# Attention weights times values: one block at a time, or four in one run, in a hybrid encoder layer

## The chip, the core and the metric

The kernel runs on one NeuronCore of a Trainium2 chip. The metric is the device time of one execution in microseconds (us). The core has a matrix engine (TensorE, PE in the profile; its weight loads are PEld), VectorE (DVE), ScalarE (ACT), GpSimd (POOL) and SyncE (SP), which issues nearly all transfers. Each engine works through its own list of instructions in order and waits on semaphores for the others.

## What is computed

The layer takes x of 1024 tokens by 1024 features and puts 16 learned meta tokens in front. Cut to what matters:

```python
u = _rmsnorm(h, norm_g[l])
z = u @ w_in[l]
gq, gk, gv, r_f, r_b, g_gate, nq, nk, nv, n_gate = jnp.split(z, split_at, axis=-1)
...  # gated linear attention (GLA) of 4 heads, one scan in each direction -> o_gla
qn = _rmsnorm(nq.reshape(B, L, NA_HEADS, NA_HEAD_DIM), q_norm_g[l])
kn = _rmsnorm(nk.reshape(B, L, NA_HEADS, NA_HEAD_DIM), k_norm_g[l])
# neighbourhood attention (NA), 16 heads of 64, per grid row of 64 tokens:
s_loc = jnp.einsum('bchd,bicjhd->bhcij', q_r, k_g) * scale   # + position bias
s_meta = jnp.einsum('bchd,bmhd->bhcm', q_r, km) * scale + mb
p = jax.nn.softmax(jnp.concatenate([s_loc.reshape(B, H, W, wh * ww), s_meta], axis=-1), axis=-1)
o = (jnp.einsum('bhcij,bicjhd->bchd', p_loc, v_g) + jnp.einsum('bhcm,bmhd->bchd', p_meta, vm))
o_na = o * jax.nn.silu(n_gate)
h = h + jnp.concatenate([o_gla, o_na], axis=-1) @ w_out[l]
```

The change touches the last product of the neighbourhood attention, weights p times values.

## The kernel before

The program has a front stage with the neighbourhood attention and a second stage with the GLA scans and the output projection. All dense products are made in a three-part form (`mm3`, L409 to L412: high by high, high by low, low by high half of each operand), so one step of 128 features is three matmuls.

**Neighbourhood attention.** The 1024 tokens are regrouped into 8 blocks of 16 grid rows by 8 columns. The 16 heads are taken as 8 pairs, numbered 0 to 7; two heads of 64 fill the 128 rows. `attn(p)` (L771) does one pair. After `k_prep` (L681), which transposes the keys (kmt, kt) and makes their halves, it goes through nine steps s = 0 to 8 (L858). In step s it

- transposes the finished weights of unit s-1 (`transposes`, L818): waits for the normalization on DVE (`norm`, L807; L814 writes P), makes three PE transposes for each of the two heads (tile pp, L825), and copies them to PT, head 0 on ACT (L829), head 1 on DVE (L831);
- starts unit s (`softmax`, L781): scores of query block s on PE (`qk`, tile s, L763 and L764), bias and row maximum on DVE (L791), exponentials on ACT (L797, L798), and the normalization deferred by 1500 and 2100 ns;
- in odd steps prepares the next two query blocks (`q_prep`, L721: PE transposes into qt, ACT copies L730, DVE L737 and POOL L741 for the other half);
- lets the dense stream run to a point inside the step (t0), then multiplies weights and values of unit s-1 (`pv`, L835), then lets the dense stream run to the end of the step (t1).

`pv` makes six matmuls, L844, from three key blocks and two heads. Each head's result has 64 rows, so head 0 uses one half of the array's columns and head 1 the other. The profile shows each of these float32 matmuls as two records, twelve for a unit. The third key block is a tile of 16 meta rows (kvm) in units 0 and 7, and VM otherwise, where the meta rows lie in the places of some tokens. Four units share one PSUM bank (po); after the fourth, L854 on DVE multiplies the bank by the gate tile ng, whose silu (ACT L648 to L651, POOL L652) is called in at the latest there (`finish(gate_rest)`, L851).

**What sets the order.** The order of instructions is made when the program is built, by `Sched` (L70). It counts ns of tensor work. The attention is the main thread; the dense stream of the next pair (`dense_na`, tiles pn_na; meta tokens pm_na; gates pz_na) is the filler, which is drawn in between by ("gap", ns) and ("to", position), and `defer` puts work of other engines a given number of ns of tensor work later. `STEP_AT` and `PV_AT` (L38, L39) place the steps and the products in the filler. ("w", 710) after `pv` says that the product counted as 710 ns. Beside the last pair runs the dense stream of the first GLA head (pz_gz, pn_gv).

**Dense evacuation.** A finished pn_na bank is read by ACT (L546, L548, L549: square, q and k, v); DVE reduces the square (L551), POOL makes the reciprocal root (L212, L213), DVE applies it (L556). Weights are split into halves by ACT and POOL (L253, L254) or DVE alone (L256, L257).

**Transfers by GpSimd.** In the GLA stage each head loads its values back with two transfers from GpSimd's queue (L1033, L1034).

Of the kernel before, what the change touches and what calls it, by code (L numbers as in the profile page):

```python
# [8 lines left out]
F32 = mybir.dt.float32  # L9
# [5 lines left out]
PSUM = bass.MemoryType.PSUM  # L15
# [11 lines left out]
# emission distances in ns of tensor work  # L27
# [9 lines left out]
LAST_NS = 3438.0  # L37
PV_AT = (0.5, 0.5, 0.5, 0.6, 0.5, 0.5, 0.5, 0.5)  # L38
# [12 lines left out]
# emission positions of block 0's parts, 8 * token block + feature block  # L51
# [8 lines left out]
# evacuations of halves that DVE does alone  # L60
# [4 lines left out]
# of four weight pieces, which ACT and Pool split  # L65
# [4 lines left out]
class Sched:  # L70
    """Orders the emission: a main thread, a filler thread and deferred work."""
# [10 lines left out]
    def defer(self, ns, fn):  # L82
        """Emits fn after ns more of tensor work, or when the returned handle is called."""
        state = []

        def once():
            if not state:
                state.append(1)
                fn()

        self.n += 1
        heapq.heappush(self.heap, (self.pe + ns, self.n, once))
        return once
# [46 lines left out]
def kernel(  # L140
# [27 lines left out]
    nc = tc.nc  # L168
# [22 lines left out]
    def pt_tile(name, hold):  # L191
        """the single bank of short-lived products, expected to be free again after hold ns."""
        S.pt_free = S.pe + hold
        return ps_tile("pt", name, 1)
# [5 lines left out]
    # ------------------------------------------------------------- constants  # L200
# [4 lines left out]
    rs = con.tile([128, 8], F32, name="rs")  # L205
# [4 lines left out]
    def rstd(dst, ss, inv_n, eng_n):  # L210
        """dst = (ss * inv_n + eps) ** -0.5 on tiny tiles."""
        pool.tensor_scalar(dst, ss, inv_n, EPS, OP.mult, OP.add)  # L212
        pool.tensor_tensor(dst, dst, epsm[: dst.shape[0], :eng_n], OP.pow)  # L213

    # ------------------------------------------------------------- weights
    pieces = []

    def add_block(key, aps, pack=1):
        """a block's pieces: each holds `pack` of its [128, columns] parts."""
        pieces.extend((key, i, pack, a) for i, a in enumerate(aps))  # L220
# [55 lines left out]
    def release(ns=0.0):  # L276
        """a piece has had its last use: the next one takes its place ns later."""
        allowed[0] += 1
        S.defer(ns, lambda: pump() if nsplit[0] < allowed[0] else None)

    # ------------------------------------------------------------- u^T
# [5 lines left out]
    # ------------------------------------------------------------- NA pools  # L287
# [20 lines left out]
    def x_load(b):  # L308
        """token block b with its features on the partitions."""
        xs[b] = zt_tile(f"x{b}")  # L310
        if b > 0:
            sp.dma_start(xs[b], xt[b])
# [5 lines left out]
    def x_rows(b):  # L318
        """token block b with its tokens on the partitions."""
        xr[b] = flat(VM if b % 2 else xv)  # L320
        sp.dma_start(xr[b], xn[b])
# [17 lines left out]
    def u_part(b, k):  # L339
        """both parts of feature block k of u^T, short of the tokens' rstd."""  # L340
        xk = xs[b][:, k * 128 : k * 128 + 128]
        ts = slice(b * 128, b * 128 + 128)
        g = gT[:, k : k + 1]
        act.activation(uh[:, k, ts], xk, AF.Copy, scale=g)
        dve.scalar_tensor_tensor(ul[:, k, ts], xk, g, f32(uh[:, k, ts]), OP.mult, OP.subtract)

    def u_split(b):
        """both parts of token block b of u^T, short of the tokens' rstd."""
        ts = slice(b * 128, b * 128 + 128)
        x3 = xs[b].rearrange("p (k t) -> p k t", k=NKB)  # L350
        halves = (slice(0, 4), slice(4, 8))
        for ks in halves:
            dve.tensor_tensor(x3[:, ks], x3[:, ks], gT[:, ks, None].to_broadcast([128, 4, 128]), OP.mult)
        for ks in halves:
            act.activation(uh[:, ks, ts], x3[:, ks], AF.Copy)  # L355
        for ks in halves:
            dve.tensor_tensor(ul[:, ks, ts], x3[:, ks], f32(uh[:, ks, ts]), OP.subtract)  # L357

    def u_rstd(b):
        """the tokens' rstd: a column of rs."""  # L360
        st = nap.tile([128, 2], F32, tag="ust", name=f"ust{b}", bufs=2)
        for i in range(2):
            junk = ps_tile("ps", f"junk{b}_{i}", 2)
            act.activation(junk, xr[b][:, 512 * i : 512 * i + 512], AF.Square, accum_out=st[:, i : i + 1])
        dve.tensor_tensor(st[:, 0:1], st[:, 0:1], st[:, 1:2], OP.add)
        rstd(rs[:, b : b + 1], st[:, 0:1], 1.0 / 1024, 1)
# [7 lines left out]
    def u_spread(b):  # L374
        """the tokens' rstd: on the free axis of all partitions."""
        ps = ps_tile("ps", f"rb{b}", 2)
        pe.matmul(ps[:, 0:128], ones, dg[b], start=True, stop=True)
        act.activation(rbc[:, b * 128 : b * 128 + 128], ps[:, 0:128], AF.Copy)
        S.adv(220)

    def u_meta():
        """um: both parts of the meta tokens' u^T."""
# [25 lines left out]
    # ------------------------------------------------------------- dense parts  # L408
# [5 lines left out]
    def first_pair(key, c1, hook):  # L414
        """token blocks 0 and 1 of the first weight block, each piece used for both as it comes."""
        ps = [ps_tile("pd", f"pn_{key[0]}{key[1]}_{b}", 2) for b in range(2)]
        for i, (b, k) in enumerate(FIRST):
            u_part(b, k)
            if (key, k) not in split:
                pump()  # L420
            hook(i)
            wh, wl, _ = split[(key, k)]
            cs = slice(b * 128, b * 128 + 128)
            mm3(ps[b][:, :c1], uh[:, k, cs], ul[:, k, cs], wh[:, :c1], wl[:, :c1], k == 0, k == NKB - 1)
            yield 3 * c1 / 2.4
        return ps

    def natural(key, b, c0, c1, pump_last=False, hooks={}, spread=0.0, tag=("pd", 2)):
        """psum[tok' of block b, columns c0:c1 of the weight block]; yields costs, returns the bank."""
# [14 lines left out]
    def transposed(key, c0, evac, pump_last=False, lag=LAG):  # L444
        """psum[128 columns from c0, 512 tokens tok'] of both halves, the second behind the first."""
# [26 lines left out]
    def seq_view(ap):  # L472
        """a [p, 1024] row-major token view, iterated in tok' order (block, row, column)."""
        return ap.rearrange("p (r b c) -> p b r c", r=16, b=8, c=8)
# [13 lines left out]
    # ------------------------------------------------------------- NA static operands  # L488
# [42 lines left out]
    # ------------------------------------------------------------- dense stream of the NA pairs  # L531
# [114 lines left out]
    def swish(g, e, ns):  # L646
        """g *= 1 / (1 + exp(-g)), with e for the second factor; the steps ns after the first."""
        act.activation(e, g, AF.Exp, scale=-1.0)  # L648
        return [
            S.defer(ns[0], lambda: act.activation(e, e, AF.Ln, bias=1.0)),  # L650
            S.defer(ns[1], lambda: act.activation(e, e, AF.Exp, scale=-1.0)),  # L651
            S.defer(ns[2], lambda: pool.tensor_tensor(g, g, e, OP.mult)),  # L652
        ]

    def run_silu():
        """the pending gates."""
# [16 lines left out]
    # ------------------------------------------------------------- neighbourhood attention  # L673
    vm_scr = dram.tile([NPAIR, 16, 128], F32, name="vm_scr")

    def v_load(p):
        """values of pair p with the meta rows in the places of each block's last column of tokens."""
# [3 lines left out]
    def k_prep(p):  # L681
        """key operands of pair p."""
# [70 lines left out]
    def span(u):  # L753
        """first block and score columns of the unit of query block u."""
        return (0 if u == 0 else u - 1), (272 if u in (0, 7) else 416)
# [15 lines left out]
    def attn(p):  # L771
# [5 lines left out]
        po = {}  # L777
        f0 = S.fill
# [39 lines left out]
        def transposes(u, Ps, norm):  # L818
            ch = ((0, 128), (144, 128), (128, 16) if u in (0, 7) else (288, 128))
            PT = []  # L820
            for a in range(2):
# [4 lines left out]
                t = nap.tile([128, 384], F32, tag="PT", name=f"PT{p}{u}{a}", bufs=4)  # L826
# [31 lines left out]
        for s in range(9):  # L858
# [19 lines left out]
            if PT is not None:  # L878
# [3 lines left out]
                pv(pu, PT)  # L882
                yield ("w", 710)
# [4 lines left out]
    # ------------------------------------------------------------- GLA: dense streams  # L888
# [5 lines left out]
    def dense_gz(h):  # L894
        """q^T and k^T of head h in row-major token order, and k^T of the meta tokens."""
# [21 lines left out]
    def r_prep():  # L917
        """[rh; rl; rh] rows of both directions' decay ranks, tokens row-major, then meta."""
# [30 lines left out]
    def dense_gv(h):  # L949
        """v of head h (bounced to row-major token order), with the decay ranks in head 0's block."""  # L950
# [42 lines left out]
    # ------------------------------------------------------------- GLA: the scans  # L993
# [29 lines left out]
    def gla(h):  # L1023
# [128 lines left out]
        def state(d, n):  # L1152
            """the chunk's own contribution k~^T v, in PSUM."""
# [116 lines left out]
    # ------------------------------------------------------------- output projection  # L1270
# [64 lines left out]
    # ------------------------------------------------------------- the whole  # L1335
# [144 lines left out]
```

## Time and profile before

| | |
|---|---|
| time, median of 3 runs | 1182.36 us (1178.92 to 1186.05) |
| profiled execution, span from first to last instruction | 1179.6 us; no other time of that execution is given |
| mean granted TensorE clock | 0.991 |
| DMA | 99.35 MB, 84 GB/s mean |

How to read it: a row of the timeline gives start and length in us, the engine, the line, the operation, the tile written and those read, the shape, and in brackets the idle time in front with what ended it. Matmuls overlap in the pipeline, so the distance between two starts tells what one costs, not its length. Equal neighbours are put in one row with their count (x4); the length is then from the first start to the last end.

### The profile page before, as it was taken

How to read it: one execution, taken by the hardware profiler on the slowest of the kernel's cores; microseconds unless marked ns; L12 is line 12 of the kernel's file. 1: busy time of each engine (PE TensorE's matmuls, PEld its weight loads, DVE VectorE, ACT ScalarE, POOL GpSimd, SP SyncE). 2: the span in 40 equal slices, each digit the busy share in tenths (PEclk: the TensorE clock that was granted, in tenths of full speed). 3: DMA queues.
4: the chain of work that ended last, by engine and by line, in shares of the span. 5: the costliest groups of instructions: out<-in, count | busy, mean ns of one | idle time of the engine just before them, and what ended most of it. 6: DMA issues, size and time to landing. Idle time of an engine off the chain costs nothing.

```text
span 1179.6 us, 18996 instructions
## 1 busy us (share of the span) xinstructions
PE 1134.1 (96%) x6739; PEld 984.9 (83%) x6739; DVE 796.3 (68%) x1995; ACT 523.2 (44%) x1363; POOL 408.0 (35%) x477
## 2 busy tenths in 40 slices
PE   9899999999999999999999799899989999999998
PEld 7789898988989898897897689689868977787876
DVE  6966767776676777677646876865576587756352
ACT  6655565655646565564544333431442144212110
POOL 4743625343352534334205332531333222202010
PEclk9999999999999999999999899999999989999999
DMA  8620303012040301203126023303512454324132
GB/s 266 212 65 2 124 2 117 10 51 75 2 124 2 117 9 52 73 2 104 36 73 192 27 75 89 123 18 91 150 30 71 119 178 147 97 56 129 49 105 106
DMA packets 74414, 99.35 MB, mean 84 GB/s; under 512 B 6672, under 2 KB 45328, under 8 KB 74320
## 3 DMA queue, kind: packets, MB, share of 16 engines
q1 hardware_dynamic: 70096, 89.75, 24.8%
q0 software_dynamic: 4224, 8.39, 2.4%
q8 instruction: 53, 0.87, 0.3%
q14 instruction: 41, 0.34, 0.1%
HBM read 72.89 MB, written 21.04 MB: 80 GB/s over the span
## 4 chain that ended last, share of the span: by engine, by line
PE 76%; DVE 14%; issue 3%; ACT 3%; POOL 2%; DMA 1%; SPq 0%; POOLq 0%; DVEq 0%; ACTq 0%
PE pn_na L410 7%; PE pn_na L411 6%; PE pn_na L412 6%; PE pout L410 4%; PE pout L412 4%; PE pout L411 4%; PE po L844 4%; PE pp L825 3%; DVE ga L1072 3%; PE pn_gv L410 3%; PE pn_gv L412 3%; PE pn_gv L411 3%; PE pz_na L410 2%; PE pz_na L412 2%; PE pz_na L411 2%
## 5 line engine op out<-in xcount | busy, mean ns | idle before, releaser
L410 PE MATMUL pn_na<-wh,uh 128*128 128x384 f32 x512 | 180.3, 352 | 0.4 <-ACT uh L355 0.3
L254 POOL TENSOR_TENSOR wl<-raw,wh 128x512 fp32r<-128x512 f32 (+2 forms) x97 | 131.2, 1366 | 128.9 <-ACT wh L253 95.6
L411 PE MATMUL pn_na<-wl,uh 128*128 128x384 f32 x512 | 174.0, 340 | 1.2 <-POOL wl L254 1.0
L412 PE MATMUL pn_na<-wh,ul 128*128 128x384 f32 x512 | 173.3, 338 | 0.1
L410 PE MATMUL pout<-wh,oh 128*128 128x512 f32 x256 | 104.4, 408 | 6.6 <-DVE acc L1331 3.6
L410 PEld LDWEIGHTS pn_na<-wh,uh 128*128 128x128 f32 x512 | 96.1, 188 | 9.0 <-issue 7.8
L412 PE MATMUL pout<-wh,oh 128*128 128x512 f32 x256 | 102.1, 399 | 0.0
L411 PE MATMUL pout<-wl,oh 128*128 128x512 f32 x256 | 102.0, 398 | 0.0
L411 PEld LDWEIGHTS pn_na<-wl,uh 128*128 128x128 f32 x512 | 96.3, 188 | 3.6 <-POOL wl L254 2.5
L412 PEld LDWEIGHTS pn_na<-wh,ul 128*128 128x128 f32 x512 | 96.1, 188 | 0.9 <-DVE ul L357 0.7
L1331 DVE TENSOR_TENSOR acc<-acc,pout 128x512 f32<-128x512 f32 x64 | 43.8, 684 | 63.7 <-PE pout L412 63.6
L797 ACT ACTIVATE P<-P,sm 128x384 f32<-128x384 f32 x96 | 58.5, 609 | 51.9 <-DVE sm L794 51.9
L410 PE MATMUL pn_gv<-wh,uh 128*128 128x256 f32 (+1 forms) x256 | 76.3, 298 | 0.0
L253 ACT ACTIVATE wh<-raw 128x512 fp32r<-128x512 f32 (+2 forms) x97 | 57.5, 608 | 37.6 <-PE pout L412 18.8
L412 PE MATMUL pn_gv<-wh,ul 128*128 128x256 f32 (+1 forms) x256 | 73.0, 285 | 0.0
L411 PE MATMUL pn_gv<-wl,uh 128*128 128x256 f32 (+1 forms) x256 | 72.9, 285 | 0.0
L212 POOL TENSOR_SCALAR post<-post 128x1 f32<-128x1 f32 x32 | 6.5, 203 | 190.5 <-ACT on L1207 190.4
L791 DVE CUSTOM_DVE_ANT_0 P<-s,wt 128x416 f32<-128x416 f32 (+1 forms) x128 | 69.5, 543 | 2.5 <-PE s L764 2.5
L213 POOL TENSOR_TENSOR ss<-ss,epsm 128x4 f32<-128x4 f32 x64 | 68.9, 1077 | 5.3
L814 DVE TENSOR_SCALAR P<-P,sm 128x384 f32<-128x384 f32 (+1 forms) x128 | 66.9, 522 | 4.5
L212 POOL TENSOR_SCALAR ss<-ss 128x4 f32<-128x4 f32 x64 | 14.1, 221 | 157.7 <-DVE ss L551 96.3
L410 PEld LDWEIGHTS pout<-wh,oh 128*128 128x128 f32 x256 | 48.6, 190 | 19.7 <-DVE gt L483 3.3
(359 smaller groups left out, 3057.9 us busy)
## 6 DMA issues: line engine op xcount, KB each, us to landing
raw<-in_w_na_dram SPq DMA_DIRECT2D x56, 256.0 KB, 2.8
v_scr<-gvst SPq DMA_DIRECT2D x64, 128.0 KB, 2.3
raw<-in_w_o_dram SPq DMA_DIRECT2D x32, 256.0 KB, 2.9
oin<-o_scr SPq DMA_DIRECT2D x32, 256.0 KB, 3.1
v<-v_scr POOLq DMA_DIRECT2D x4, 1536.0 KB, 9.2
VM<-vnat SPq DMA_DIRECT2D x8, 512.0 KB, 4.5
o_scr<-ng SPq DMA_DIRECT2D x8, 512.0 KB, 3.5
raw<-in_w_gz_dram SPq DMA_DIRECT2D x16, 256.0 KB, 2.7
```

The costliest lines, as they stand in the source:

```text
L213: pool.tensor_tensor(dst, dst, epsm[: dst.shape[0], :eng_n], OP.pow)
L253: act.activation(wh[:, :n], r[:, :n], AF.Copy)
L254: pool.tensor_tensor(wl[:, :n], r[:, :n], f32(wh[:, :n]), OP.subtract)
L410: pe.matmul(ps, ah, bh, start=start, stop=False)
L411: pe.matmul(ps, ah, bl, start=False, stop=False)
L412: pe.matmul(ps, al, bh, start=False, stop=stop)
L791: dve.tensor_tensor_reduce(P[:, :n], ps[:, :n], wt[2 * p + a][:, off : off + n], 1.0, -3.0e38, OP.add, OP.max, mx)
L797: act.activation(loc, loc, AF.Exp, bias=mx, accum_out=sm[:, a : a + 1])
L814: dve.tensor_scalar(loc, loc, r, None, OP.mult)
L825: pe.transpose(pp[:w, c * 128 : c * 128 + 128], Ps[a][0][:, c0 : c0 + w], ident)
L844: pe.matmul(po[0][64 * a : 64 * a + 64, u4 * 128 : u4 * 128 + 128], V[:, 64 * a : 64 * a + 64], PT[a][:w, c * 128 : c * 128 + 128], start= ...
L1331: dve.tensor_tensor(a, a, ps, OP.add)
```

## The change

- `attn` collects the finished units in a list, `ready`, and calls `pv` for four of them in one run when the list is full, in steps 4 and 8. The run counts as 4 x 654 + 56 ns of tensor work.
- The pool for PT has eight buffers instead of four.
- The program is built with a scratch of 4096 bytes for descriptors of GpSimd's transfers, instead of the default.

Comments and docstrings were taken out as well, so line numbers move a little.

```diff
+PV_BATCH = 4
...
         po = {}
+        ready = []
...
-                t = nap.tile([128, 384], F32, tag="PT", name=f"PT{p}{u}{a}", bufs=4)
+                t = nap.tile([128, 384], F32, tag="PT", name=f"PT{p}{u}{a}", bufs=8)
...
                 if s == 1:
                     for m in vload:
                         m()
-                pv(pu, PT)
-                yield ("w", 710)
+                ready.append((pu, PT))
+                if len(ready) == PV_BATCH:
+                    for r in ready:
+                        pv(*r)
+                    yield ("w", 654 * PV_BATCH + 56)
+                    ready.clear()
             if s < 8:
                 yield ("to", t1)
...
-    nc = _bacc.Bacc("TRN2", target_bir_lowering=False, num_devices=1)
+    nc = _bacc.Bacc("TRN2", target_bir_lowering=False, num_devices=1, dynamic_dma_scratch_size=4096)
```

On PE, in step 5 of the first pair, the program before had unit 4's product (L844, tile po) between matmuls of the dense stream (pn_na_5):

```order
L410 MATMUL pn_na_5_1335<-wh_699,uh 128x384
L411 MATMUL pn_na_5_1335<-wl_700,uh 128x384
L412 MATMUL pn_na_5_1335<-wh_699,ul 128x384
L844 MATMUL po_1358<-PT_1294,vnat_137 64x128
L844 MATMUL po_1358<-PT_1300,vnat_137 64x128
L844 MATMUL po_1358<-PT_1294,vnat_137 64x128
L844 MATMUL po_1358<-PT_1300,vnat_137 64x128
L844 MATMUL po_1358<-PT_1294,VM 64x128
L844 MATMUL po_1358<-PT_1300,VM 64x128
L410 MATMUL pn_na_5_1335<-wh_713,uh 128x384
```

Now the dense matmuls there follow each other, and the products stand in runs; this is the middle of the run in step 4 of the same pair, on PE, from the end of unit 0 over unit 1 to the start of unit 2 (kvm holds the meta values, VM and vnat values of tokens):

```order
L847 MATMUL po_1251<-PT_948,kvm_639 64x128
L847 MATMUL po_1251<-PT_955,kvm_639 64x128
L847 MATMUL po_1251<-PT_1036,vnat_137 64x128
L847 MATMUL po_1251<-PT_1042,vnat_137 64x128
L847 MATMUL po_1251<-PT_1036,vnat_137 64x128
L847 MATMUL po_1251<-PT_1042,vnat_137 64x128
L847 MATMUL po_1251<-PT_1036,VM 64x128
L847 MATMUL po_1251<-PT_1042,VM 64x128
L847 MATMUL po_1251<-PT_1127,vnat_137 64x128
L847 MATMUL po_1251<-PT_1133,vnat_137 64x128
```

Nothing else moves on PE: without the rows of po both programs have the same matmuls in the same order. DVE and SP have the same order as before. On POOL one instruction of each pair moves; before, with ng the gate tile, Q query halves and ss sums of squares:

```order
L741 TENSOR_SCALAR Q_012_1172<-Q_10_97 64x256
L652 TENSOR_TENSOR ng_743<-ng_743,sig_975 128x1024
L212 TENSOR_SCALAR ss_3_1214<-ss_3_1214 128x4
L213 TENSOR_TENSOR ss_3_1214<-ss_3_1214,epsm 128x4
L212 TENSOR_SCALAR ss_4_1327<-ss_4_1327 128x4
```

and now, on POOL, at the same place:

```order
L743 TENSOR_SCALAR Q_012_1159<-Q_10_97 64x256
L214 TENSOR_SCALAR ss_3_1194<-ss_3_1194 128x4
L215 TENSOR_TENSOR ss_3_1194<-ss_3_1194,epsm 128x4
L654 TENSOR_TENSOR ng_743<-ng_743,sig_975 128x1024
L214 TENSOR_SCALAR ss_4_1327<-ss_4_1327 128x4
```

The gate's last multiply stands behind one pair of ss instructions instead of in front of it. On ACT one step of the gate's silu (tile sig) moves in the same way, behind the four exponentials of unit 2 in pairs 0 to 6, and behind a copy to PT in pair 7.

## The prediction

> **What bounds the kernel now.** I read the busy shares first, then the chain of waits, then the rows of TensorE (PE) around the products of attention weights and values, then, for each of the eight steps of a pair, which wait ends last before PE goes on.
>
> ```profile
> PE 1134.1 (96%) x6739; PEld 984.9 (83%) x6739; DVE 796.3 (68%) x1995; ACT 523.2 (44%) x1363; POOL 408.0 (35%) x477
> PE 76%; DVE 14%; issue 3%; ACT 3%; POOL 2%; DMA 1%; SPq 0%; POOLq 0%; DVEq 0%; ACTq 0%
> ```
>
> PE is busy 96% of the span and holds 76% of the chain; VectorE (DVE) holds 14%. So PE time is worth saving where no DVE wait stands right behind it. Here is one product of one query block (unit 2 of the first pair) between two matmuls of the dense stream:
>
> ```profile
> 94.18 0.33 PE L412 MATMUL pn_na<-wh,ul 128*128 128x384 f32 x1
> 94.44 0.66 PE L844 MATMUL po<-PT,vnat 128*64 128x128 f32 x8
> 94.93 0.39 PE L844 MATMUL po<-PT,VM 128*64 128x128 f32 x4
> 95.25 0.44 PE L410 MATMUL pn_na<-wh,uh 128*128 128x384 f32 x1
> 95.53 0.34 PE L411 MATMUL pn_na<-wl,uh 128*128 128x384 f32 x1
> 95.70 0.34 PE L412 MATMUL pn_na<-wh,ul 128*128 128x384 f32 x1
> ```
>
> Matmuls overlap, so starts are what counts. Two dense starts lie 0.17 to 0.18 us apart (95.53 to 95.70). The twelve records of L844 run as six pairs, one for each half of the array's columns, 0.11 us apart: 0.65 us of work. Yet from 94.18 to 95.53 there is 1.35 us, where 0.175 + 0.65 + 0.175 = 1.00 would do. So a unit pays about 0.35 us for going into the half-width shape and out of it: the first L844 comes 0.26 after its forerunner instead of 0.175, the next dense matmul is followed only after 0.28 (95.25 to 95.53).
>
> **The change part by part.** *Removed.* Of eight units of a pair, six lose their place between dense matmuls (0, 1, 2, 4, 5, 6); units 3 and 7 keep theirs, at the end of a run of four. Unit 0 multiplies by the 16 meta values (tile kvm), unit 1 lies in front of the meta matmuls:
>
> ```profile
> 148.21 0.33 PE L412 MATMUL pn_na<-wh,ul 128*128 128x384 f32 x1
> 148.47 0.66 PE L844 MATMUL po<-PT,vnat 128*64 128x128 f32 x8
> 149.06 0.43 PE L844 MATMUL po<-PT,kvm 16*64 16x128 f32 x4
> 149.42 0.44 PE L410 MATMUL pn_na<-wh,uh 128*128 128x384 f32 x1
> 149.70 0.34 PE L411 MATMUL pn_na<-wl,uh 128*128 128x384 f32 x1
> ...
> 86.57 0.33 PE L412 MATMUL pn_na<-wh,ul 128*128 128x384 f32 x1
> ...
> 87.64 0.32 PE L468 MATMUL pm_na<-wh,um 128*48 128x256 f32 x1
> 87.79 0.28 PE L469 MATMUL pm_na<-wl,um 128*48 128x256 f32 x1
> ```
>
> Unit 0: 149.70 - 148.21 = 1.49, less two plain steps (0.35) is 1.14. Unit 1: 87.79 - 86.57 = 1.22, less 0.175 and the 0.12 between meta matmuls, is 0.93. Unit 2 gives 1.35 - 0.35 = 1.00, and units 4, 5, 6 are of the same shape. Sum 1.14 + 0.93 + 4 x 1.00 = 6.07 us a pair.
>
> *Added.* The same six units inside the runs, at 0.65 each: 3.92. Unit 0 takes 1.49 where unit 2 takes 1.35, and its pairs on kvm start 0.59 after the first L844 where those on VM start 0.49 after it (148.47 to 149.06, 94.44 to 94.93): 0.10 to 0.14 for the change to 16 rows. Inside a run unit 1 then changes back. No row shows that way back; between nothing and a whole entry and exit (0.35) I take 0.15, the way in rounded up, which is nearest, so 0.30 in all (ends: 1.2 us less or 1.6 us more over eight pairs). Added 4.22; PE's own balance is 6.07 - 4.22 = -1.85 us a pair.
>
> *What is late next.* The page gives PE 96% and its weight loads (PEld) 83%. The Trainium skill ("Perfetto Trace Analysis", Identifying the Most-Contended Engine) calls matmul busy time a poor measure and asks for weight-load time instead. Read by the 96%, all of PE's balance would come off the time, 14.9 us in eight pairs; read by the waits below, nothing does.
>
> The balance counts only where PE isn't stopped before it has used the time. In step s PE transposes the weights of unit s-1, computes the scores of unit s, runs dense matmuls, in the middle of them the product of unit s-1, and at the next step needs the finished weights of unit s. This softmax hangs on PE's scores, which lie ahead of the product. A product taken out of the step brings PE sooner to a wait whose other side has not moved. I take the steps one by one, with 0.15 us as the least distance from a DVE end to the PE start that waited for it (467.25 to 467.40 in the rows of step 7).
>
> In steps 1 and 2 DVE is done ahead of PE by more than the saving; 1.14 and 0.93 are kept. Step 3 (unit 2 goes), in the fifth pair:
>
> ```profile
> 371.22 0.87 DVE L737 TENSOR_TENSOR Q<-qt,Q 64x256 fp32r<-64x256 f32 x2
> 372.18 0.44 PE L763 MATMUL s<-K,Q 128*128 128x416 f32 x1
> ```
>
> The first of the two L737 ends at 371.22 + 0.43 = 371.65; the score matmul that reads it starts at 372.18, 0.53 later. Kept: 0.53 - 0.15 = 0.38 of 1.00. Step 5 (unit 4 goes):
>
> ```profile
> 378.60 0.56 DVE L831 COPY PT<-pp 128x384 f32<-128x384 f32 x1 [0.73 <-PE pp L825]
> 383.26 0.42 DVE L551 TENSOR_REDUCE ss<-sq 128x4 f32<-128x256 f32 x1 [2.71 <-ACT sq L546]
> 384.75 0.49 DVE L814 TENSOR_SCALAR P<-P,sm 128x384 f32<-128x384 f32 x1
> 385.27 0.87 DVE L737 TENSOR_TENSOR Q<-qt,Q 64x256 fp32r<-64x256 f32 x2
> 385.14 0.82 PE L825 MATMUL pp<-ident,P 128*128 128x128 f32 x6
> 385.83 0.43 PE L763 MATMUL s<-K,Q 128*128 128x416 f32 x1
> ```
>
> DVE waits 2.71 us for one ScalarE (ACT) square, which is queued behind the exponentials; behind it stand both normalizations (L814) and both L737. The first L737 ends at 385.27 + 0.43 = 385.70, and PE's score matmul, due right behind the six transposes, starts at 385.83: PE is at this wait already. The stretch hangs on PE's transposes of the step before (the wait at 378.60), ahead of the product that goes, so nothing of 1.00 is kept. Step 6 (unit 5 goes) and step 7 (unit 6 goes):
>
> ```profile
> 390.85 0.48 DVE L814 TENSOR_SCALAR P<-P,sm 128x384 f32<-128x384 f32 x1
> 391.99 0.82 PE L825 MATMUL pp<-ident,P 128*128 128x128 f32 x6
> ...
> 395.74 0.69 DVE L257 TENSOR_TENSOR wl<-raw,wh 128x512 fp32r<-128x512 f32 x1
> 396.54 1.20 DVE L814 TENSOR_SCALAR P<-P,sm 128x272 f32<-128x272 f32 x1
> 397.86 0.82 PE L825 MATMUL pp<-ident,P 128*128 128x128 f32 x6
> ...
> 464.14 1.82 DVE L257 TENSOR_TENSOR wl<-raw,wh 128x512 fp32r<-128x512 f32 x1
> 466.07 1.18 DVE L814 TENSOR_SCALAR P<-P,sm 128x272 f32<-128x272 f32 x1
> 467.40 0.52 PE L825 MATMUL pp<-ident,P 128*128 128x128 f32 x3 [0.67 <-DVE P L814]
> ```
>
> The second three transposes start 0.33 after the first three. Step 6: L814 ends at 391.33, they start at 392.32; kept 0.84. Step 7 has two forms. In the pairs 0, 1 and 4 L814 ends at 397.74, the transposes start at 398.19; kept 0.30. In the pairs 2, 3, 5 and 6 the weight split L257 takes 1.82 instead of 0.69, L814 ends at 467.25, and PE already waits for it; kept nothing.
>
> Steps 4 and 8 hold the runs, 4.22 us more in all. In the pairs of the first form PE now waits at the end of step 8 as well, for the last normalized row block:
>
> ```profile
> 403.94 1.41 PE L692 MATMUL kt<-ident,nat 128*128 128x128 f32 x8
> 403.48 1.48 DVE L556 TENSOR_TENSOR nat<-nat,ss 128x256 f32<-128x256 f32 x1 [1.18 <-POOL ss L213]
> ```
>
> Eight transposes at 0.11 take 1.04 with the last one's length; 1.41 leaves about 0.3 of waiting, which the longer run in front covers.
>
> *Sum.* Pairs 0, 1, 4: kept 1.14 + 0.93 + 0.38 + 0 + 0.84 + 0.30 = 3.59; 4.22 - 3.59 - 0.3 = +0.33 us. Pairs 2, 3, 5, 6: kept 3.29, +0.93 us. The last pair runs beside GLA blocks and is looser: between all kept (-1.9) and the others (+0.9) I take the middle, -0.5. Together 3 x 0.33 + 4 x 0.93 - 0.5 = +4.2 us. The profiled span is 1179.6; the median, 1182.36, is 2.8 above it, which I carry over: 1186.6 us.
>
> *Edits at no cost.* Eight PT buffers (L826): a buffer is written again only after the run that read it. The DVE order is the same in both programs; the multiply at L854 waits 2 us longer for the run's end, with only L556 ahead of the next copy behind it, and PE's own next transposes are later by as much. GpSimd's ng multiply (L652) moves behind one ss pair, one step of ACT's sig behind exponentials; their only hurried reader is L854. The smaller scratch touches eight transfers of GpSimd:
>
> ```profile
> v<-v_scr POOLq DMA_DIRECT2D x4, 1536.0 KB, 9.2
> ```
>
> The four vx transfers (L1034) go with them. They are issued ahead of a head's decay work, which hides them; a second wait of the same 9.2 us would still lie under it. Bound: nothing to 2 us.
>
> **The rivals.** *PE alone sets the time* (all 1.85 us kept in seven pairs, 1.9 in the last): 1182.4 - 14.9 = 1167.5. For it: 96%. Against it: the rows of steps 5 and 7, where PE already stands at a DVE end. Chance 0.12. A half-way case, in which the DVE stretch of step 5 or 7 moves forward too, gives about 1176; chance 0.05.
>
> *The split is slow in every pair* (ends slower). In step 7 L257 starts at 395.74 or 464.14 within 0.01 us of a GpSimd split:
>
> ```profile
> 464.13 4.27 POOL L254 TENSOR_TENSOR wl<-raw,wh 128x512 fp32r<-128x512 f32 x3 [0.52 <-ACT wh L253]
> ```
>
> If the first three forms fall to the slow side, L814 ends 1.1 us later there: 3 x 1.1 = 3.3 more, 1189.9 us; it decides from two of the three pairs on (2.2 more). Going to the fast side everywhere gives 4 x 1.1 less, 1182, inside my case. "SBUF — State Buffer" (Who interferes with whom) of the Trainium skill says that DVE with two SBUF inputs and a reading GpSimd hold a port in turn and whoever is first keeps it; by that rule the form is a toss-up, and the trace's 0.69 against 1.82 agrees. Chance 0.27.
>
> *The change doesn't do what it says*: the array leaves its shape between the units of a run. Six times 0.35 a pair comes back, less the 0.15 counted: 8 x 1.95 = 15.6 more, 1202. Against it: six pairs of one unit already run at 0.11. Chance 0.03.
>
> **How the numbers follow.** My case, the DVE-bound steps give nothing back, has 0.53 and spans 1180 to 1188; I predict 1186.6. A measurement of this kernel tells 0.5% (5.9 us) from no change, so faster means below 1176.4 and slower above 1188.3. Faster: 0.12 and half of 0.05, with a little for a sum that is off, 0.15. Slower: 0.27 and 0.03, 0.30. Same: 0.55. Range 1174 to 1192: my case with the ends of the kvm term, the slow split with 1.6 on top, and the half-way case; it leaves out the full gain and the last rival.
>
> **What would show it.** Right: units of a run 0.65 apart; PE's waits for P (L814) and for Q (L737) in steps 3, 5, 6 and 7 grow from almost nothing to about 0.6, 1.0, 0.2 and 0.7 to 1.0 us a pair; the pair's period changes by under 1 us. Wrong: the period falls by 1.5 us or more with no new waits on PE, or the span changes behind the last pair, in GLA.

## The result, and the profile after

The changed kernel takes 1197.8 us (median of 4 runs, 1193.4 to 1198.8) where the kernel before took 1181.5 in the runs beside it: ratio 1.0123, 95% interval 1.0098 to 1.0148. The forecast was 1186.6, no more than 1192. The profiled execution took 1197.1 us with a span of 1195.3, 15.7 more than the span before (forecast: 4.2). One execution of a later kernel (the profiled one of e9) ran 2786 us, more than twice as long as its other six, with the dense matmuls of L412 at 689 ns where those of L410 before take 352, and is left out. Busy shares and the chain of waits of the changed kernel:

```profile
PE 1131.6 (95%) x6739; PEld 987.6 (83%) x6739; DVE 805.2 (67%) x1995; ACT 523.4 (44%) x1363; POOL 407.5 (34%) x477
PE 66%; DVE 19%; ACT 9%; issue 4%; DMA 1%; POOL 1%; SPq 0%; DVEq 0%; ACTq 0%; POOLq 0%
```

PE does the same instructions in slightly less busy time, and its part of the chain falls from 76 to 66%; DVE's rises from 14 to 19, ACT's from 3 to 9. The saved PE time has become waiting. First the run itself, in the second pair (start, duration, engine and line; lines of the changed kernel are 2 or 3 higher than before):

```profile
168.97 0.33 PE L414 MATMUL pn_na<-wh,ul 128*128 128x384 f32 x1
169.24 0.66 PE L847 MATMUL po<-PT,vnat 128*64 128x128 f32 x8
169.82 0.43 PE L847 MATMUL po<-PT,kvm 16*64 16x128 f32 x4
170.19 0.66 PE L847 MATMUL po<-PT,vnat 128*64 128x128 f32 x8
170.67 0.39 PE L847 MATMUL po<-PT,VM 128*64 128x128 f32 x4
170.89 0.61 PE L847 MATMUL po<-PT,vnat 128*64 128x128 f32 x8
...
171.55 0.61 PE L847 MATMUL po<-PT,vnat 128*64 128x128 f32 x8
...
172.30 0.44 PE L412 MATMUL pn_na<-wh,uh 128*128 128x384 f32 x1
172.58 0.34 PE L413 MATMUL pn_na<-wl,uh 128*128 128x384 f32 x1
```

From 168.97 to 172.58 are 3.61 us, against 1.35 for the one unit that stood here: 2.26 more. Full-width units lie 0.66 apart (170.89 to 171.55), and the array is entered and left once. The other run, between the gate's dense matmuls (pz_na) and the next pair's kmt, costs 1.96 more. Together 4.23 us a pair, where the forecast had 4.22. So the part that the change is about came out as worked out. The waits did not. The list of what PE waited for, over the whole span (total, times, longest), has this row for the kernel before:

```profile
PE pp L825 <- DVE P L814: 2.7, 4, 0.7
```

and these for the changed kernel:

```profile
PE pp L828 <- DVE P L817: 18.2, 21, 1.7
PE pp L828 <- ACT P L801: 1.4, 7, 0.2
```

21 waits are three in each of seven pairs, in the steps 3, 5 and 7 (0.64, 0.26 and 1.70 us in the second pair). Here is the largest, in step 7 of the second pair, first on DVE, then on POOL, then on PE:

```profile
191.50 0.41 DVE L258 CAST wh<-raw 128x512 fp32r<-128x512 f32 x1
191.95 1.66 DVE L259 TENSOR_TENSOR wl<-raw,wh 128x512 fp32r<-128x512 f32 x1
...
193.73 1.17 DVE L817 TENSOR_SCALAR P<-P,sm 128x272 f32<-128x272 f32 x1
```

```profile
191.73 4.30 POOL L256 TENSOR_TENSOR wl<-raw,wh 128x512 fp32r<-128x512 f32 x3 [0.31 <-ACT wh L255]
```

```profile
192.86 0.49 PE L828 MATMUL pp<-ident,P 128*128 128x128 f32 x3
195.05 0.52 PE L828 MATMUL pp<-ident,P 128*128 128x128 f32 x3 [1.70 <-DVE P L817]
```

DVE's weight split takes 1.66 us, and in the changed kernel it does so in step 7 of every one of the seven pairs (1.66 to 1.67); before it took 0.69 there in three pairs and 1.82 in four. PE's second three transposes come 2.19 us after the first three instead of 0.33 in this pair before.

The second is in step 3, and is new: PE waits here for both heads' weights of unit 3, where before it waited for neither.

```profile
165.03 0.52 PE L828 MATMUL pp<-ident,P 128*128 128x128 f32 x3 [0.20 <-ACT P L801]
166.19 0.52 PE L828 MATMUL pp<-ident,P 128*128 128x128 f32 x3 [0.64 <-DVE P L817]
166.64 0.43 PE L765 MATMUL s<-K,Q 128*128 128x416 f32 x1
```

I lined up the PE matmuls of both traces (all but those of the products, which are the same in the same order) and took how much the distance between two neighbours grew. In step 3 of the second pair the growth at the six transposes and the scores is 0.36 + 0.80 + 0.18 + 0.08 = 1.42 us; the forecast was 0.62. The same count for the pair, product and waits together, in us:

| step | forecast, pairs 0, 1, 4 | measured, pair 1 | forecast, pairs 2, 3, 5, 6 | measured, pair 2 |
|---|---|---|---|---|
| 1 | -1.14 | -1.14 | -1.14 | -1.14 |
| 2 | -0.93 | -0.90 | -0.93 | -0.90 |
| 3 | -0.38 | +0.42 | -0.38 | +0.42 |
| 5 | 0 | -0.11 | 0 | -0.11 |
| 6 | -0.84 | -0.82 | -0.84 | -0.82 |
| 7 | -0.30 | +0.87 | 0 | +0.03 |
| runs (4, 8) | +4.22 | +4.23 | +4.22 | +4.23 |
| end of step 8 (kt) | -0.3 | -0.28 | 0 | 0 |
| pair's period | +0.33 | +2.43 | +0.93 | +1.92 |

(The rest of the period, 0.16 and 0.21, is made of jumps under 0.06.) Seven pairs give 14.9 of the 15.7 us, the last pair -0.7 up to the end of its second run, and what lies behind it, in the GLA stage, about +1.4. Two cells are wrong: step 3 everywhere, by 0.80, and step 7 in three pairs, by 1.17.

In step 3 I looked for what comes later on ACT. The sequence behind unit 2's exponentials in the changed kernel:

```profile
157.14 0.19 ACT L801 ACTIVATION_READ_ACCUMULATOR P<-P,sm 128x1 f32 x1
157.23 1.04 ACT L652 ACTIVATE sig<-sig 128x1024 f32<-128x1024 f32 x1
158.18 0.45 ACT L548 ACTIVATE sq<-pn_na,rs 128x256 f32<-128x256 f32 x1
...
159.28 0.38 ACT L567 ACTIVATE kvt<-pm_na 16x256 f32<-16x256 f32 x1
```

and in the kernel before:

```profile
152.56 1.05 ACT L650 ACTIVATE sig<-sig 128x1024 f32<-128x1024 f32 x1
...
155.78 0.19 ACT L798 ACTIVATION_READ_ACCUMULATOR P<-P,sm 128x1 f32 x1
155.87 0.46 ACT L546 ACTIVATE sq<-pn_na,rs 128x256 f32<-128x256 f32 x1
...
158.17 0.38 ACT L565 ACTIVATE kvt<-pm_na 16x256 f32<-16x256 f32 x1 [1.23 <-PE pm_na L469]
```

Before, the sig step lay ahead of unit 2's exponentials, and ACT then stood idle 1.23 us for PE's meta matmuls (pm_na). Now the sig step lies behind the exponentials and ACT does not wait at all. What hangs on kvt, into which ACT copies part of the meta tokens' keys and values, is long: kvm, kvs and kvm again on ACT, DVE and POOL, and behind them on DVE, in its fixed order, the scores of unit 3, their exponentials and norms. PE waits for these at the end of step 3.

From this came the theory of two places. One: the moved sig step makes unit 3's chain late, about 0.8 us a pair. Two: the split is slow in step 7 of all pairs. The rivals: the buffers or the scratch cost the time; the chains are late whatever the order is, only because PE's own cover went.

### The profile page after: what moved, and what is told of

It is laid out like the page before. It is cut to its first block, busy times and chain, and to the rows that moved or that the text cites. A ratio compares the mean times of both kernels' runs of the same rounds, so it can differ in the third digit from the quotient of the medians.

```text
span 1195.3 us, 19008 instructions
## 1 busy us (share of the span) xinstructions
PE 1131.6 (95%) x6739; PEld 987.6 (83%) x6739; DVE 805.2 (67%) x1995; ACT 523.4 (44%) x1363; POOL 407.5 (34%) x477
## 4 chain that ended last, share of the span: by engine, by line
PE 66%; DVE 19%; ACT 9%; issue 4%; DMA 1%; POOL 1%; SPq 0%; DVEq 0%; ACTq 0%; POOLq 0%
PE pout L412 4%; PE pout L414 4%; PE pout L413 4%; PE po L847 4%; PE pn_na L412 4%; PE pn_na L413 4%; PE pn_na L414 4%; PE pp L828 3%; DVE ga L1079 3%; ACT P L800 3%; PE pz_na L412 2%; PE pz_na L414 2%; PE pn_gv L412 2%; PE pz_na L413 2%; PE pn_gv L413 2%
## 5 line engine op out<-in xcount | busy, mean ns | idle before, releaser
L412 PE MATMUL pn_na<-wh,uh 128*128 128x384 f32 x512 | 177.5, 347 | 1.4 <-ACT uh L357 0.3
L412 PE MATMUL pout<-wh,oh 128*128 128x512 f32 x256 | 104.4, 408 | 6.5 <-DVE acc L1338 2.9
L412 PEld LDWEIGHTS pn_na<-wh,uh 128*128 128x128 f32 x512 | 96.2, 188 | 6.2 <-ACT vnat L551 3.2
L828 PE MATMUL pp<-ident,P 128*128 128x128 f32 (+1 forms) x384 | 58.3, 275 | 19.8 <-DVE P L817 18.2
L412 PE MATMUL pn_gv<-wh,uh 128*128 128x256 f32 (+1 forms) x256 | 76.0, 297 | 0.6 <-ACT rst L979 0.6
```

Of the source, the lines that this page charges most:

```text
L412: pe.matmul(ps, ah, bh, start=start, stop=False)
L828: pe.transpose(pp[:w, c * 128 : c * 128 + 128], Ps[a][0][:, c0 : c0 + w], ident)
```

## The experiments

Each kernel was timed beside the kernel before on the same chip; ratios are to that, with 95% intervals. "The changed kernel" stands for its 1197.8 us, measured apart from the experiments. By the intervals of the ratios a difference to it is uncertain by 3 to 4 us; what it is made of is read from the traces.

**Runs of one (e1_runs_of_one).** Only the buffers and the scratch are left of the change; the instructions of each engine stand in the order of before.

```diff
-PV_BATCH = 4
+PV_BATCH = 1
-                    yield ("w", 654 * PV_BATCH + 56)
+                    yield ("w", 710)
```

> The changed kernel with runs of one product, so that only the eight PT buffers and the smaller scratch are left of the change; the order of every engine is that of the kernel before. The two places theory (the runs cost PE what was worked out; the rest of the loss is one ACT step moved in front of unit 3's chain, 0.80 us in each of seven pairs, and the weight split of step 7, slow in every pair, 1.1 us in three pairs): as before, 1181.5 us, within 2. Rival, the scratch or the buffers cost time: between 1184 and 1197, all or part of the 16 us.

Measured: 1182.6 us beside 1182.9, ratio 1.0004 (0.9994 to 1.0014). Buffers and scratch cost nothing; all of the loss is in how the products are issued.

The trace of this kernel shows one thing more. With the same order as before, the split of step 7 was fast in six of the seven pairs of this execution and slow in one, where the kernel before had three and four. On DVE, in the first and in the second pair:

```profile
121.50 1.83 DVE L259 TENSOR_TENSOR wl<-raw,wh 128x512 fp32r<-128x512 f32 x1
...
190.44 0.69 DVE L259 TENSOR_TENSOR wl<-raw,wh 128x512 fp32r<-128x512 f32 x1
```

So the mix of the two forms does not follow from the order alone.

**The sig step put back (e2_sig_back).** The changed kernel, with the first two deferrals of the silu steps shorter, so that ACT's order is that of before.

```diff
-SIG_NS = (6480.0, 10000.0, 16000.0)
+SIG_NS = (5770.0, 10000.0, 16000.0)
```

> The changed kernel with the first two later steps of the gate's silu issued so early that ACT's order is that of the kernel before; POOL's stays changed, PE's runs stay. Two places theory: unit 3's chain (kvt, kvs, scores, exponentials, norms) is 0.80 us earlier, PE's wait in step 3 falls from 1.42 to 0.62 us a pair, 7 x 0.80 = 5.6 us less than the changed kernel: 1192. Rival, the chain is late whatever ACT's order is, since only PE's own cover went: no change, 1197.5 and a wait of 1.4.

Measured: 1192.4 us, 1.0084 (1.0066 to 1.0102), 5.4 less than the changed kernel (4.6 by the two ratios). PE in step 3 of the second pair, in that kernel:

```profile
164.36 0.49 PE L828 MATMUL pp<-ident,P 128*128 128x128 f32 x3
165.11 0.52 PE L828 MATMUL pp<-ident,P 128*128 128x128 f32 x3 [0.26 <-DVE P L817]
165.56 0.43 PE L765 MATMUL s<-K,Q 128*128 128x416 f32 x1
```

The first three transposes no longer wait, the second three come 0.75 after them instead of 1.16, and the growth of step 3 is 0.67, near the 0.62 of the forecast. So one ACT instruction, in another place of ACT's queue, was worth 0.75 us a pair, 5.3 in seven. Step 7 keeps its 1.86.

**The sig step moved in the kernel before (e3_sig_moved_in_before).** The counterpart: ACT in the order of the changed kernel, nothing else.

```diff
-SIG_NS = (6480.0, 10000.0, 16000.0)
+SIG_NS = (7190.0, 10000.0, 16000.0)
```

> The kernel before with ACT's sig step moved behind unit 2's exponentials as in the changed kernel, and nothing else on any engine. Two places theory: unit 3's chain is 0.80 us later; PE had 0.53 - 0.15 = 0.38 us to spare at the scores of unit 4, so it waits about 0.4 us in each of seven pairs, 2.9 us in all: 1184.4. Rival, ACT's order does not matter: 1181.5, no wait.

Measured: 1181.4 us beside 1182.9, ratio 0.9990 (0.9980 to 1.0000): no loss, as the rival had it. My expectation was wrong, and the group of kvt on ACT in that kernel (busy, mean ns, then the idle time ahead and what ended it) says why:

```profile
L565 ACT ACTIVATE kvt<-pm_na 16x256 f32<-16x256 f32 x1 | 0.4, 377 | 0.3 <-PE pm_na L469 0.3
```

The sig step fits into the 1.23 us for which ACT waits for the meta matmuls; 0.3 are left and kvt is not late. So the extra 0.75 of step 3 comes neither from the order alone nor from the products' release alone (which leaves 0.67), but from both together: taking unit 1's product (0.90) from in front of the meta matmuls used up most of that idle time, and the sig step, put into the same place, no longer fits. In the changed kernel with the sig step back, the same row reads:

```profile
L567 ACT ACTIVATE kvt<-pm_na 16x256 f32<-16x256 f32 x1 | 0.4, 377 | 0.1
```

**The split of step 7 off DVE (e4_split_off_dve).** In six of the seven pairs ACT and POOL split the piece that DVE split in step 7.

```diff
-            if (NA1_ACT[j - 8] if 8 <= j < 16 else SPLIT_ACT[key[0]][j % 4]):
+            if (NA1_ACT[j - 8] if 8 <= j < 16 else SPLIT_ACT[key[0]][j % 4] or (key[0] == "na" and j >= 16 and j % 8 == 3)):
```

> The changed kernel with the weight piece that DVE splits in step 7 split by ACT and POOL instead, in six of the seven pairs. Two places theory: 0.41 + 1.66 = 2.07 us go from DVE in front of unit 7's norms, so PE's wait there (1.9 us behind where it could be in the pairs 0, 1 and 4, and as long in the others) falls to under 0.3: about 6 x 1.6 to 1.8 = 10 us less than the changed kernel, 1187. Rival, what takes the split over becomes late next (POOL's wl in front of the next dense matmuls, or ACT's exponentials behind one more cast): less than half of that, 1193 or more.

Measured: 1188.5 us, 1.0052 (1.0038 to 1.0065), 9.3 less than the changed kernel (8.4 by the ratios). PE's waits in it:

```profile
PE pp L828 <- DVE P L817: 8.0, 15, 1.7
PE pp L828 <- ACT P L801: 1.4, 7, 0.2
```

Six of the 21 waits are gone and 10.2 us of the 18.2: the six of step 7, 1.7 each. The one of 1.7 that is left is the seventh pair's, where the piece was not moved.

**Both edits (e5_sig_and_split).** The split as in e4, and the silu steps put back, the third too, so that POOL's order is also that of before.

```diff
-SIG_NS = (6480.0, 10000.0, 16000.0)
+SIG_NS = (5770.0, 10000.0, 14500.0)
```

> The changed kernel with both edits: the silu steps issued so that ACT and POOL have the order of before, and step 7's weight piece off DVE. Two places theory: two separate waits, so the gains add, 5.4 + 9.3 us from the changed kernel's 1197.8: 1183. Rival, both are waits of one chain and the second gives less once the first is gone: 1187 or more.

Measured: 1181.9 us, 0.9993 (0.9977 to 1.0009). The gains add, 15.9 us against 5.4 + 9.3, within the uncertainty. With both, the changed kernel is where the kernel before is.

**The split off DVE in the kernel before (e8_split_off_dve_in_before).** The same edit of the split as in e4. Its ACT, POOL, DVE and SP orders are those of the kernel with both edits; only PE's products stand singly.

> The kernel before with step 7's weight piece off DVE in the same six pairs. Theory (the split is off the path where PE has a product to do meanwhile): PE hardly waits there, 0 to 0.5 us a pair, so 0 to 2 us less than before, 1180 to 1182. Rival, the split costs the same in both kernels: 9 us less, 1173.

Measured: 1186.3 us, 1.0023 (1.0006 to 1.0041). An edit that gave 9.3 us in the changed kernel costs 3.6 here against the 1182.7 beside it. The forecast of little gain was right in its first half (PE waits for P fall by 2.0 us), but a new wait came, first in PE's list and then on DVE and POOL:

```profile
PE kt L692 <- DVE nat L556: 4.9, 6, 0.9
PE pp L825 <- DVE P L814: 0.7, 1, 0.7
```

```profile
200.35 1.48 DVE L556 TENSOR_TENSOR nat<-nat,ss 128x256 f32<-128x256 f32 x1 [1.18 <-POOL ss L213]
```

```profile
191.85 6.78 POOL L254 TENSOR_TENSOR wl<-raw,wh 128x512 fp32r<-128x512 f32 x5 [0.52 <-ACT wh L253]
198.71 0.52 POOL L212 TENSOR_SCALAR ss<-ss 128x4 f32<-128x4 f32 x1
```

POOL has one split more ahead of the last row block's ss, and PE waits for the block at the pair's end (kt). In the kernel with both edits a run of four stands in front of kt, and the wait is in its list once:

```profile
PE kt L694 <- DVE nat L558: 0.9, 1, 0.9
```

Apart from buffers and scratch, which cost nothing (e1), the two kernels differ only in PE's products, so here the runs are worth 4.4 us (1186.3 to 1181.9, side by side on one chip; 3.5 by the means).

**Cover moved (e10_cover_moved_alone, e6_cover_moved).** One group of three dense matmuls more in step 3 and in step 5, both from step 4, which holds a run; the run goes behind unit 4's norms. With it one row block's norm on DVE (L558) moves four instructions ahead in all seven pairs. Once in the changed kernel as it is, once with both edits.

```diff
-PV_AT = (0.5, 0.5, 0.5, 0.6, 0.5, 0.5, 0.5, 0.5)
-STEP_AT = (0.78, 2.0, 3.0, 4.0, 4.92, 6.0, 7.08, 8.0)
+PV_AT = (0.5, 0.5, 0.5, 0.6, 0.8, 0.5, 0.5, 0.5)
+STEP_AT = (0.78, 2.0, 3.0, 4.15, 4.77, 6.0, 7.08, 8.0)
```

> The changed kernel with the moved cover alone (one group of dense matmuls more in step 3 and one in step 5, both from step 4, whose run goes behind unit 4's norms); ACT's sig step and DVE's split stay as the changed kernel has them. Theory: the waits of steps 3 and 5 shrink by 0.53 each a pair, those of step 7 stay: 7 x 1.05 = 7 us less than the changed kernel, 1190. Rival, the late chain of step 3 moves with the dense work: no gain, 1197.

Measured: 1189.6 us, 1.0072 (1.0058 to 1.0086), 8.2 less than the changed kernel (6.0 by the ratios). In the traces the second pair's period falls from 70.85 to 69.79 us, 0.53 in each of the two steps. In step 5 most of that, 0.40, is a wait for a bank that ACT empties late (its row stands in the next section), which no longer occurs.

> The kernel with both edits, and beside them one group of three dense matmuls more in step 3 and one more in step 5, both taken from step 4, which holds a run and has about 2.1 us to spare; step 4's run goes behind the norms of unit 4. Theory (PE's release is lost only because the steps without a product have too little other PE work to cover their softmax): the waits of step 3 (0.67) and step 5 (0.9) shrink by 0.53 each, 7 x 1.05 = 7 us less than the kernel with both edits: 1176. Rival, the chain of the step begins later too when more dense work (and its evacuations on ACT and DVE) lies in it: no gain, 1183.

Measured: 1175.3 us, 0.9935 (0.9913 to 0.9957), 6.6 less than with both edits. What is left of PE's waits for P:

```profile
PE pp L828 <- DVE P L817: 1.9, 2, 1.7
```

A chain behind PE is not bound to be late; it is late when its step holds too little else for PE to do. Dense work put where the product was taken out does what the product did, without changing the array's shape. Whether the same move would also speed up the kernel before, with its single products, was not run, so the 0.6% of this kernel is that of the move and the runs together.

**Runs of 3, 1, 1, 2, 1 (e7_runs_3_1_1_2_1).** ACT and DVE have the order of the changed kernel; only the places of the runs change, and with them the gate's last multiply on POOL, which in the pairs 0 to 6 is back at its place of before.

```diff
-PV_BATCH = 4
+PV_RUNS = (3, 1, 1, 2, 1)
-                if len(ready) == PV_BATCH:
+                if pu + 1 in [sum(PV_RUNS[:i + 1]) for i in range(len(PV_RUNS))]:
...
-                    yield ("w", 654 * PV_BATCH + 56)
+                    yield ("w", 654 * len(ready) + 56)
```

> The changed kernel with runs of 3, 1, 1, 2 and 1 products instead of 4 and 4: units 0 to 2 in step 3, 3 and 4 alone in their steps, 5 and 6 in step 7, 7 in step 8; ACT's sig step stays where the changed kernel has it. Theory: runs lie in the steps in which PE waits; steps 1 and 2 keep 1.14 + 0.90, step 3 pays 1.61 and covers the late chain, step 6 keeps 1.00 - 0.17, step 7 pays 0.65 against a wait for the split: 0.6 us a pair less than before, 8 x 0.6 = 4.9: 1177 (ratio 0.996). Rival, runs themselves cost (the wait follows the run wherever it is): 1184 or more.

Measured: 1175.7 us, 0.9936 (0.9914 to 0.9959). In the traces seven pairs give 6.6 us of it. ACT's sig step stands as in the changed kernel, but step 3 now has a run in front of its end. Unit 3's norms on DVE and the transposes that read them, second pair:

```profile
162.35 0.48 DVE L817 TENSOR_SCALAR P<-P,sm 128x384 f32<-128x384 f32 x1
163.38 0.61 DVE L817 TENSOR_SCALAR P<-P,sm 128x384 f32<-128x384 f32 x1
```

```profile
165.23 0.82 PE L828 MATMUL pp<-ident,P 128*128 128x128 f32 x6
```

The norms end at 162.83 and 163.99, 2.4 us before the first three transposes and 1.6 before the second three (0.33 behind them), where in the changed kernel PE waited for both. The chain is as late as there (kvt on ACT starts 6.46 us after the first transposes of step 2 in both) and costs nothing.

**One step further (e9_cover_moved_further).** As e6, and one more group from step 4 to step 5, one from step 5 to step 6.

```diff
-STEP_AT = (0.78, 2.0, 3.0, 4.15, 4.77, 6.0, 7.08, 8.0)
+STEP_AT = (0.78, 2.0, 3.0, 4.15, 4.57, 5.9, 7.08, 8.0)
```

> The kernel with both edits and the moved cover, and one more group of three dense matmuls taken from step 4 (which still has 1.9 us to spare) for step 5, one of step 5's last for step 6; DVE's sum of squares of step 5 comes behind unit 5's norms. Theory: the waits left in step 5 (about 0.4) and step 6 (0.17) go, 0.3 to 0.5 us a pair, 2 to 3 us less: 1172.5. Rival, the kernel is now at PE's own work and only the order on ACT and POOL changes: 1175, or more if a row block's norm becomes late for the next pair.

Measured: 1173.0 us (median of six), 0.9929 (0.9913 to 0.9945), the fastest; the step from e6 is no larger than the intervals, so whether the waits left in the steps 5 and 6 went is not shown.

## Why the prediction was wrong, point by point

- *Price of the shape.* Right. 0.35 us to go in and out of half width: removed 42.4 us in seven pairs (forecast 6.07 x 7 = 42.5), the runs added 29.6 (forecast 29.5). The rival by which the array leaves its shape inside a run is out.
- *Kept nothing behind a DVE end.* Right in kind, and in size for steps 1, 2, 5, 6 and the kt wait, to 0.11. In step 5 the growth is 0.89 (forecast 1.00), made otherwise than I said: 0.50 is the wait for unit 5's weights, 0.40 a wait for a bank which ACT empties late. PE's weight loads in the changed kernel show that one:

```profile
180.69 0.19 PEld L412 LDWEIGHTS pn_na<-wh,uh 128*128 128x128 f32 x1 [0.45 <-ACT vnat L551]
```

- *Edits at no cost: one step of ACT's sig behind exponentials, whose only hurried reader is L854.* This is the step that failed. I asked who reads the sig step and not what stands behind it on ACT: the square, nat, vnat and kvt, and by kvt the whole softmax of unit 3. I also read step 3 from the end (a slack of 0.53 at the scores) as if its start would stay, while step 2's own saving had moved PE's meta matmuls 0.90 towards ACT and so removed the idle time that would have taken the sig step in. The term "kept 0.38" was in truth -0.42. Seven times 0.80 is 5.6 us; the sig step put back gave 5.4, and 0.75 a pair in its trace.
- *The split is slow in every pair* (rival, chance 0.27, 1189.9). This came true: 3 x 1.17 = 3.5 us more. In my chosen case the old mix of forms was simply carried over, although the price of the other outcome was known, and although the order does not fix the mix: e1, in the same order, had six fast pairs of seven.
- *Last pair and GLA.* Forecast -0.5; measured -0.7 for the pair up to the end of its second run. Behind it came about +1.4, for which the sum has no term. One execution can't tell a cause there: in the trace of e1, whose instructions stand in the order of before, the same stretch is 1.5 us longer than in before's, and over the kernels with the same dense order on PE it differs by -2.0 (e7) to +2.0 us (e2).

Sum: 4.2 + 5.6 (step 3) + 3.5 (split) + 1.2 (last pair and what lies behind it) - 0.8 (step 5) + 0.4 (steps 2 and 6, runs) + 1.3 (jumps under 0.06) is 15.4 of the 15.7. The range's top, 1192, held the rival but no term for a moved ACT step, so the two together lay outside. By the rival "PE alone sets the time" the kernel should have gained 15; with both waits mended and the cover moved it gained 7.4 (e6), half of that.

What is shown: the cost of the sig step (put back, -5.4), that PE's waits of step 7 hang on the split (taken off, -9.3), and that with both edits the loss is gone (0.9993). The 9.3 is more than the 3.5 which the slow form adds: taking the piece off DVE also ends the waits of 0.67 that four pairs had before, and those that the product taken out of step 7 had covered. So e5 does not take back the losses one by one, and the kernel to hold it against is e8, which has the same split and no runs. What is argued only: why POOL leads DVE in step 7 of every pair. It is not the sig step, since POOL leads by the same 0.21 us in e2. In the changed kernel the norm ahead of the split takes 0.76 us beside POOL's previous piece, 0.55 before, and DVE comes to the split about 0.2 us after POOL; no run tested that alone.

## What to carry to other kernels

A stretch of work on a busy engine is worth its time only if nobody uses it as cover: before taking it out of a step, list what the engine waits for at that step's end, and put other ready work there or leave the stretch where it is. When an emission schedule counts the work that you move, look at the order of every engine, and for each instruction that changes place ask what is queued behind it, not only who reads it. And place runs in the steps in which the engine waits, not at equal counts: 3, 1, 1, 2, 1 gained 0.6% where 4, 4 lost 1.2%.

## What the hardware showed

The durations of both splits go with which of DVE and POOL starts first. Of the seven pairs of the kernel before, in three DVE started level or 1 ns ahead, and took 0.69 us and POOL 1.84; in four POOL was 9 to 12 ns ahead, and DVE took 1.82 and POOL 1.28. In e1 POOL is 7 ns ahead in the one slow pair, and in the six fast ones DVE starts from 3 ns ahead to 1 ns behind. In the changed kernel POOL is 0.21 us ahead in every pair, and DVE takes 1.66 each time. "SBUF — State Buffer" (Who interferes with whom) of the Trainium skill calls the shared port pair an exclusive lock; these rows agree with it, with the price beside it: the one that comes second waits out most of its partner's piece. A norm on DVE (128x272) takes 0.36 us where no split of POOL runs beside it, and up to 1.20 (before) or 1.50 (e4) where one does.

Changing the row count inside a run costs little: from 128 to 16 rows 0.10 us (169.24 to 169.82 is 0.58, against 0.48 for 170.19 to the VM rows), and back 0.15 (169.82 to 170.19 is 0.37, against 0.22 from VM to the next unit), together 0.25 where I had taken 0.30. That the sum of the runs still met the forecast to 0.01 us is therefore in part luck.
